# Gate and up products of a SwiGLU from seven block products where eight were formed

## The chip, the cores and the metric

The kernel runs on one core of one Trainium2 chip. Its time is device microseconds (us) from the start to the end of one execution. The engines are TensorE (PE in the profile, its weight loads PEld), VectorE (DVE), ScalarE (ACT), GpSimd (POOL) and SyncE (SP), which here only issues transfers. The operands of products lie in SBUF, the results in the banks of PSUM.

## The reference

One layer of a streaming encoder on 2080 tokens (a prompt of 2048 and a sample of 32) with 1024 features. In front are four mixers between two projections; the change is in what follows them:

```python
        f = rms_norm(x, g_ffn[l])
        hid = jax.nn.silu(jnp.einsum('bld,df->blf', f, w_gate[l])) * jnp.einsum('bld,df->blf', f, w_up[l])
        x = x + jnp.einsum('blf,fd->bld', hid, w_down[l])
...
    y = rms_norm(x, g_final)
```

The hidden width is 2816. All values are float32.

## The kernel before, in words

**Layout.** Features lie on the 128 partitions (8 tiles of 128, `KT`), tokens along the columns, in 5 chunks of 416 (`C`). `x2[c]` holds the running sum of a chunk.

**Exactness.** TensorE takes a format with fewer bits (`F32R`). So every operand is split into a rounded part hi and a rest lo, and `product` (L215 to L223) forms hi·hi, hi·lo and lo·hi: three matmuls of 128 x 128 x 416 for each tile of the contraction, on lines 221, 222 and 223. The hi part of a weight is a ScalarE copy (L128), the lo part a GpSimd subtraction (L129).

**SwiGLU.** The 2816 hidden features are 22 blocks of 128 (`NFB`). `FFN_PASSES` takes chunks 0, 1, 2 in a first pass over all blocks and 3, 4 in a second, so weights are loaded and split twice. For a block and a chunk, `gate` is 24 matmuls and a Silu on ScalarE (L940), `up` 24 matmuls, a VectorE multiplication (L948), a ScalarE copy to hi (L951) and a GpSimd subtraction to lo (L952). `down` is 3 matmuls for each of the 8 output tiles, and VectorE adds each result to `x2` (L862). The downs of a block are queued by `down_later` and issued by `run_downs` between the gates and ups of the next block, a whole gate or more after their operands were begun. Gate, up and down share five PSUM banks (`ps_mm`); three more (`ps_ax`) serve sums.

**What orders the work.** VectorE and TensorE run in the order in which the program is written (`MANUAL`); the other engines' order is chosen by a planner that may move a step ahead. Work that isn't on the way to the next product (norms, statistics, the next chunks' operands) is written as generators in the list `ahead`. After a product the program calls `fill(budget)`, which takes steps from the first `active[0]` generators until their stated VectorE times use up the budget; `WAIT` ends a generator's turn at this product, `LATE` puts a step behind the others. `need` runs what is left of a generator at once.

**Norms.** `ffn_stats` (squares on ScalarE L189, sums on VectorE L190, the sum over partitions by small matmuls L138, a power on GpSimd L154) gives the scale of each token. `spread_far` brings it to all partitions by way of DRAM (L176 out, L178 back). `f_of` makes a chunk's normed hi and lo parts straight from `x2` (L202, L205, L198). `finish` does the last norm of a chunk the same way (L883) and writes it. The last chunk's tokens are taken in two parts of 208 columns (`downs_last`, L905), so that the first part's norm runs beside the second part's products.

## Time and profile before

| | |
|---|---|
| three timed runs | 2201.39, 2204.69 (median), 2205.53 us |
| profiled execution, span from first to last instruction | 2191.8 us, 12.9 under the median |
| mean granted TensorE clock | 0.986 |
| first gate product, end of the last product of SwiGLU | 667.4 us, 2178.3 us |
| PE, DVE, POOL, ACT busy | 2123.2, 1127.5, 696.6, 510.9 us |
| moved by DMA | 147.22 MB, mean 67 GB/s |

The profile gives no separate time of the profiled execution beside its span; what lies around the span is taken as the 12.9 us to the median. In rows by line the columns are: line, engine, operation, result <- operands, shapes, count, then busy time and mean ns of one, then idle time of the engine ahead of them and what ended it. "min/median/max" rows give the spread of one group. Timeline rows give the start, the length, the engine and the line, with the idle time ahead in brackets. A matmul's recorded length (about 350 ns) is longer than its share of the time, since matmuls overlap; the step from one start to the next is what counts.

### The profile page before, as it was taken

To read this page: it belongs to the slowest core of one execution; us is meant where nothing else is said; L and a number is where in the kernel's file an instruction comes from. 1 tells how busy PE (TensorE), PEld (TensorE's weight loads), DVE (VectorE), ACT (ScalarE), POOL (GpSimd) and SP (SyncE) were. 2 spreads that over 40 slices of the span, in tenths; PEclk is the share of its full clock that TensorE was granted. 3 is DMA by queue.
4 is the path that set the end of the run, shared out by engine and by line. 5 is a ranking of instruction groups with operands and counts; after the bars stand their busy time and mean duration, and the time that the engine had idled before them with its cause. 6 is when DMAs were issued, how large, how long until landed. Compare 5 with 4: busy or idle time off the path is not lost.

```text
span 2191.8 us, 27451 instructions
## 1 busy us (share of the span) xinstructions
PE 2123.2 (97%) x11164; PEld 2076.0 (95%) x11164; DVE 1127.5 (51%) x1723; ACT 510.9 (23%) x788; POOL 696.6 (32%) x399
## 2 busy tenths in 40 slices
PE   8799999999889999999999999999999999999998
PEld 7699988899889999999999999999999999999997
DVE  3886598599446433333333333334766533333335
ACT  5324223322423211111111111111322111111123
POOL 2433253243233222222231231232333333333333
PEclk9899999999999999999999999999999999999998
DMA  7534132113321111111111111111122211111111
GB/s 224 165 94 113 63 122 70 48 58 120 113 62 53 39 39 39 39 39 39 39 39 39 39 39 39 39 43 43 48 86 93 93 58 59 59 61 61 60 49 63
DMA packets 54911, 147.22 MB, mean 67 GB/s; under 512 B 14817, under 2 KB 24801, under 8 KB 53633
## 3 DMA queue, kind: packets, MB, share of 16 engines
q1 hardware_dynamic: 52065, 145.29, 20.6%
q8 instruction: 87, 1.43, 0.3%
q10 hardware_dynamic: 2720, 0.18, 0.1%
q14 instruction: 39, 0.32, 0.1%
HBM read 136.77 MB, written 8.68 MB: 66 GB/s over the span
## 4 chain that ended last, share of the span: by engine, by line
PE 80%; DVE 11%; DMA 5%; issue 2%; POOL 1%; ACT 1%; SPq 0%; DVEq 0%; ACTq 0%; POOLq 0%
PE pu L223 7%; PE pu L221 7%; PE pd L222 7%; PE pd L223 7%; PE pg L223 7%; PE pd L221 7%; PE pu L222 7%; PE pg L221 7%; PE pg L222 7%; PE ps L221 4%; PE ps L223 4%; DVE cv L688 4%; PE ps L222 4%; DMA line<-rt 2%; DVE f L202 2%
## 5 line engine op out<-in xcount | busy, mean ns | idle before, releaser
L129 POOL TENSOR_TENSOR wlo<-raw,whi 128x1024 fp32r<-128x1024 f32 x199 | 502.8, 2529 | 854.2 <-ACT whi L128 709.9
L862 DVE TENSOR_TENSOR x<-pd,x 128x416 f32<-128x416 f32 x864 | 491.0, 591 | 432.7 <-PE pd L223 432.7
L221 PE MATMUL pd<-hhi,whi 128*128 128x416 f32 (+1 forms) x896 | 311.2, 347 | 3.0 <-ACT sg L940 2.3
L222 PE MATMUL pd<-hhi,wlo 128*128 128x416 f32 (+1 forms) x896 | 312.8, 349 | 0.0
L223 PE MATMUL pd<-hlo,whi 128*128 128x416 f32 (+1 forms) x896 | 312.1, 348 | 0.2 <-DVE hlo L952 0.2
L223 PE MATMUL pg<-flo,whi 128*128 128x416 f32 x880 | 310.1, 352 | 0.0
L223 PE MATMUL pu<-flo,whi 128*128 128x416 f32 x880 | 309.9, 352 | 0.0
L221 PE MATMUL pu<-fhi,whi 128*128 128x416 f32 x880 | 309.2, 351 | 0.0
L221 PE MATMUL pg<-fhi,whi 128*128 128x416 f32 x880 | 308.9, 351 | 0.0
L222 PE MATMUL pu<-fhi,wlo 128*128 128x416 f32 x880 | 307.8, 350 | 0.0
L222 PE MATMUL pg<-fhi,wlo 128*128 128x416 f32 x880 | 307.5, 349 | 0.0
L128 ACT CAST whi<-raw 128x1024 fp32r<-128x1024 f32 (+1 forms) x205 | 211.9, 1035 | 268.0 <-PE ps L223 111.3
L948 DVE TENSOR_TENSOR sg<-pu,sg 128x416 f32<-128x416 f32 x110 | 65.0, 591 | 396.0 <-PE pu L223 395.9
L952 POOL TENSOR_TENSOR hlo<-sg,hhi 128x416 fp32r<-128x416 f32 x109 | 120.0, 1101 | 436.0 <-ACT hhi L951 435.8
L221 PE MATMUL ps<-hi,whi 128*128 128x416 f32 x640 | 235.6, 368 | 8.3 <-ACT hi L205 4.1
L222 PE MATMUL ps<-hi,wlo 128*128 128x416 f32 x640 | 229.1, 358 | 5.8 <-POOL wlo L129 5.1
L223 PE MATMUL ps<-lo,whi 128*128 128x416 f32 x640 | 230.4, 360 | 2.9 <-POOL lo L198 2.5
L688 DVE SCALAR_TENSOR_TENSOR cv<-z,par,cv 128x416 f32<-128x416 f32 (+2 forms) x180 | 209.9, 1226 | 1.0 <-ACT cv L682 0.8
L951 ACT CAST hhi<-sg 128x416 fp32r<-128x416 f32 x110 | 59.5, 541 | 596.4 <-DVE sg L948 587.9
L221 PEld LDWEIGHTS pd<-hhi,whi 128*128 128x128 f32 x896 | 168.4, 188 | 6.9 <-ACT sg L940 3.0
L223 PEld LDWEIGHTS pd<-hlo,whi 128*128 128x128 f32 x896 | 168.3, 188 | 1.8 <-DVE hlo L952 0.3
L222 PEld LDWEIGHTS pd<-hhi,wlo 128*128 128x128 f32 x896 | 168.3, 188 | 1.5
(140 smaller groups left out, 2719.7 us busy)
## 6 DMA issues: line engine op xcount, KB each, us to landing
raw<-in_w_gate SPq DMA_DIRECT2D x44, 512.0 KB
raw<-in_w_up SPq DMA_DIRECT2D x44, 512.0 KB
raw<-in_w_down SPq DMA_DIRECT2D x44, 512.0 KB
raw<-in_w_in SPq DMA_DIRECT2D x43, 512.0 KB
raw<-in_w_out SPq DMA_DIRECT2D x24, 512.0 KB
xt<-in_xt SPq DMA_DIRECT2D x20, 416.0 KB
x<-in_x SPq DMA_DIRECT2D x5, 1664.0 KB
xk<-in_x SPq DMA_DIRECT2D x32, 208.0 KB
```

Of the source, the lines that this page charges most:

```text
L128: nc.scalar.copy(out=hf[:, o], in_=raw[:, o])
L129: lo_eng.tensor_sub(out=lf[:, o], in0=raw[:, o], in1=hf[:, o].bitcast(F32))
L202: nc.vector.scalar_tensor_tensor(out=f, in0=x(k), scalar=col(gname, k), in1=r[:, :C], op0=ALU.mult, op1=ALU.mult)
L221: nc.tensor.matmul(out, whi, xhi, start=start and k == 0, stop=False)
L222: nc.tensor.matmul(out, wlo, xhi, start=False, stop=False)
L223: nc.tensor.matmul(out, whi, xlo, start=False, stop=stop and k == n - 1)
L688: nc.vector.scalar_tensor_tensor(out=cv[:, t, :n], in0=z[:, t, j : j + n], scalar=col("w_conf", 31 * t + j), in1=cv[:, t, :n], op0=ALU.mul ...
L862: nc.vector.tensor_add(out=x2[c][:, m], in0=ps[:, :C], in1=x2[c][:, m])
L948: nc.vector.tensor_mul(out=sg, in0=ps[:, :C], in1=sg)
L951: nc.scalar.copy(out=hi, in_=sg)
L952: lo_eng.tensor_sub(out=lo, in0=sg, in1=hi.bitcast(F32))
```

## The change

The gate and the up projection of two feature blocks and two token chunks together are a product of 2 x 2 blocks: the 1024 inputs in two halves (`H` = 4 tiles each), the outputs in two blocks of 128, the tokens in two chunks. Formed plainly that is eight block products. The change forms seven (p1 to p7), of sums and differences of the weight blocks and of the operand's blocks, and puts the four results together from them.

- The tokens are cut into six chunks of 346 to 348 (`FCH`), in three passes of two; so weights are loaded and split three times.
- `operands` makes the seven weight operands of a pair of feature blocks: four sums of 512 columns on VectorE, seven splits (ScalarE, GpSimd). They are made three products ahead (`LEAD`).
- `halves` makes the seven operands of the tokens: four scalings and four differences per tile on VectorE, seven splits whose lo parts alternate between GpSimd and VectorE. The normed rows are read back from DRAM (`x2d`), where `ffn_stats` now stores `x2`. In the first pass the parts of p3 are made last, because their place is free only when the mixers' buffers are closed. The operands of the second and third pass are made when all pairs of the pass before are written, beside its last 16 downs.
- `block` forms the seven products in four PSUM banks. p2, p3 and p4 are added in PSUM onto p1, p5 and p7, after VectorE or ScalarE has read those. `evac` is called for each of the four quadrants; three of them add a partial sum (`u2`, `u3`) on VectorE.
- `up` multiplies three quadrants on GpSimd, and the lo part of all four is now a VectorE subtraction.
- `down` contracts both feature blocks into one bank: six matmuls and one VectorE addition. Downs now use the three banks of `ps_ax`. `DOWNS` says how many follow each of the 14 products of a pair; the first follows the first product.
- The running sum of a pass (`residual`) is loaded from `x2d` after the first pair of that pass, into the buffers of the two chunks before, after these have been finished.
- The end is rewritten: the last two chunks' downs follow one another, the first one's `finish` is filled in beside the second one's downs, and the second's norm follows.

The core of the diff:

```diff
+FCH = (348, 348, 346, 346, 346, 346)
...
+FPASSES = ((0, 1), (2, 3), (4, 5))
+NG = NFB // 2
+H = KT // 2
+ORDER = ("p1", "p5", "p7", "p6", "p2", "p3", "p4")
+DOWNS = (1, 1, 2, 1, 1, 2, 1, 1, 2, 1, 1, 2, 0, 0)
+LEAD = 3
...
-FFN_PASSES = ((0, 1, 2), (3, 4))
...
+    x2d = dramp.tile([P, KT, T], F32, tag="x2d", name="x2d", bufs=1)
...
+        nc.sync.dma_start(out=x2d[:, :, c * C : (c + 1) * C], in_=x2[c])
...
+    def halves(p):
+        for c in STATS_OF[p]:
+            need(("fstats", c))
+        n = FCH[FPASSES[p][0]]
+        r = []
+        for c in FPASSES[p]:
...
+        yield WAIT
+        f[p] = {}
+        engs = [nc.gpsimd, nc.vector]
+        def split(name, kk, src):
...
+            nc.scalar.copy(out=hi[:, kk, :n], in_=src)
+            engs[0].tensor_sub(out=lo[:, kk, :n], in0=src, in1=hi[:, kk, :n].bitcast(F32))
+            engs.append(engs.pop(0))
+        def normed(i, k):
+            c = FPASSES[p][i]
+            x = rowf("xf")[:, :n]
+            nc.sync.dma_start(out=x, in_=x2d[:, k, FO[c] : FO[c] + n])
+            nc.vector.scalar_tensor_tensor(
+                out=x, in0=x, scalar=col("g_ffn", k), in1=r[i][:, :n], op0=ALU.mult, op1=ALU.mult
+            )
+            return x
+        for kk in range(H):
+            f11 = normed(0, kk)
+            yield 0.8
+            split("p1", kk, f11)
+            f12 = normed(1, kk)
+            yield 0.8
+            t1 = rowf("t1")[:, :n]
+            nc.vector.tensor_sub(out=t1, in0=f12, in1=f11)
+            split("p5", kk, t1)
+            yield 1.0
+            f22 = normed(1, kk + H)
+            yield 0.8
+            t2 = f11
+            nc.vector.tensor_sub(out=t2, in0=f22, in1=t1)
+            t3 = t1
+            nc.vector.tensor_sub(out=t3, in0=f22, in1=f12)
+            split("p7", kk, t3)
+            yield 1.6
+            split("p6", kk, t2)
+            f21 = normed(0, kk + H)
+            yield 1.2
+            split("p2", kk, f21)
...
+            t4 = f12
+            nc.vector.tensor_sub(out=t4, in0=f21, in1=t2)
+            split("p4", kk, t4)
+            yield 1.0
+        if p == 0:
+            yield HOLD
+            for kk in range(H):
+                f22 = normed(1, kk + H)
+                yield 0.8
+                split("p3", kk, f22)
...
+    early = itertools.takewhile(lambda s: s is not HOLD, made["f", 0])
+    ahead.append(early)
+    for _ in w_out_pass(2):
+        pass
+    for _ in early:
+        pass
...
+    mixers.close()
+    f3 = ctx.enter_context(tc.tile_pool(name="f3", bufs=1, reuse_waits="tile"))
...
+    fw = ctx.enter_context(tc.tile_pool(name="fw", bufs=5, reuse_waits="tile"))
+    hidp = ctx.enter_context(tc.tile_pool(name="hidp", bufs=10, reuse_waits="tile"))
...
+    def weight_parts(src, tag="w", **bufs):
+        hi = fw.tile([P, H, P], F32R, tag=tag + "hi", name="whi", **bufs)
+        lo = fw.tile([P, H, P], F32R, tag=tag + "lo", name="wlo", **bufs)
...
+        nc.scalar.copy(out=hf, in_=src)
+        nc.gpsimd.tensor_sub(out=lf, in0=src, in1=hf.bitcast(F32))
+        return hi, lo
+    def operands(src, g):
+        r1, r2 = raw_of(src, g, 0), raw_of(src, g, 1)
+        a11, a21, a12, a22 = r1[:, 0], r1[:, 1], r2[:, 0], r2[:, 1]
...
+        yield weight_parts(a11)
+        s1 = total(a21, a22, add=True)
+        yield weight_parts(s1)
+        yield weight_parts(total(a11, a21))
+        s2 = total(s1, a11)
+        yield weight_parts(s2)
+        yield weight_parts(a12)
+        yield weight_parts(total(a12, s2))
+        yield weight_parts(a22)
...
+        def take(self, step):
+            self.upto(step + LEAD)
+            return self.done.pop(step)
...
+    def wide(w, x, n, ps, start, stop):
...
+        for k in range(H):
+            nc.tensor.matmul(ps, whi[:, k], xhi[:, k, :n], start=start and k == 0, stop=False, **more)
+            nc.tensor.matmul(ps, wlo[:, k], xhi[:, k, :n], start=False, stop=False, **more)
+            nc.tensor.matmul(ps, whi[:, k], xlo[:, k, :n], start=False, stop=stop and k == H - 1, **more)
...
+    def down(c, m, w, hid):
+        n = FCH[c]
+        ps = ps_ax.tile([P, 512], F32, tag="ax", name="pd")[:, :n]
+        for i, ((whi, wlo), (hhi, hlo)) in enumerate(zip(w, hid)):
+            nc.tensor.matmul(ps, whi[:, m % H], hhi[:, :n], start=i == 0, stop=False)
+            nc.tensor.matmul(ps, wlo[:, m % H], hhi[:, :n], start=False, stop=False)
+            nc.tensor.matmul(ps, whi[:, m % H], hlo[:, :n], start=False, stop=i == 1)
+        nc.vector.tensor_add(out=xs[c][:, m, :n], in0=ps, in1=xs[c][:, m, :n])
...
+    def block(p, evac):
+        n = FCH[FPASSES[p][0]]
+        bank = {}
+        def out(name):
+            bank[name] = ps_mm.tile([P, 512], F32, tag="mm", name="pw")[:, :n]
+            return bank[name]
+        def form(name, ps, start, stop):
+            w = wq.take(step[0])
+            wide(w, f[p][name], n, ps, start, True)
+        def then(k):
+            run_downs(DOWNS[step[0] % 14])
+            step[0] += 1
+        form("p1", out("a"), True, False)
+        fill(0.9)
+        r1 = rowf("r1")[:, :n]
+        nc.scalar.copy(out=r1, in_=bank["a"])
+        then(0)
+        form("p5", out("d"), True, False)
+        fill(1.0)
+        then(1)
+        form("p7", out("e"), True, False)
+        fill(0.6)
+        then(2)
+        form("p6", out("b"), True, True)
+        fill(0.6)
+        u2 = rowf("u2")[:, :n]
+        nc.vector.tensor_add(out=u2, in0=bank["b"], in1=r1)
+        u3 = rowf("u3")[:, :n]
+        nc.vector.tensor_add(out=u3, in0=bank["e"], in1=u2)
+        evac((1, 1), bank["d"], u3)
+        then(3)
+        form("p2", bank["a"], False, True)
+        fill(0.3)
+        evac((0, 0), bank["a"], None)
+        then(4)
+        form("p3", bank["d"], False, True)
+        fill(0.6)
+        evac((0, 1), bank["d"], u2)
+        then(5)
+        form("p4", bank["e"], False, True)
+        fill(0.6)
+        evac((1, 0), bank["e"], u2)
+        then(6)
+    def ffn_pair(p, g):
...
+        def gate(q, ps, plus):
+            s = rowf("sg")[:, :n]
+            if plus is not None:
+                nc.vector.tensor_add(out=s, in0=ps, in1=plus)
+                ps = s
+            nc.scalar.activation(out=s, in_=ps, func=AF.Silu)
+            sg[q] = s
+        def up(q, ps, plus):
+            s = sg[q]
+            if plus is not None:
+                u = rowf("up")[:, :n]
+                nc.vector.tensor_add(out=u, in0=ps, in1=plus)
+                nc.gpsimd.tensor_mul(out=s, in0=u, in1=s)
+            else:
+                nc.vector.tensor_mul(out=s, in0=ps, in1=s)
+            hi = hidp.tile([P, FN], F32R, tag="hid", name="hhi")
+            lo = hidp.tile([P, FN], F32R, tag="hid", name="hlo")
+            nc.scalar.copy(out=hi[:, :n], in_=s)
+            nc.vector.tensor_sub(out=lo[:, :n], in0=s, in1=hi[:, :n].bitcast(F32))
+            hid[q] = hi, lo
+        block(p, gate)
+        block(p, up)
+        return hid
...
+        order = [(m, i) for m in range(KT) for i in range(2)]
+        if by_chunk:
+            order = [(m, i) for i in range(2) for m in range(KT)]
+        for m, i in order:
+            downs.append(
+                lambda m=m, i=i: down(FPASSES[p][i], m, wd(m // H), [hid[0, i], hid[1, i]])
+            )
...
+    def finish(c):
+        n = FCH[c]
+        x = xs[c]
+        acc = rowf("ssum")
+        whole(acc, n)
+        for k in range(KT):
+            sq = acc if k == 0 else rowf("sq")
+            nc.scalar.activation(out=sq[:, :n], in_=x[:, k, :n], func=AF.Square)
+            if k:
+                nc.vector.tensor_add(out=acc[:, :n], in0=acc[:, :n], in1=sq[:, :n])
+            yield 0.8
+        yield WAIT
+        tok = ps_ax.tile([P, 512], F32, tag="ax", name="tok")
+        for j in range(FNB):
+            sums(tok[:FTB, j : j + 1], acc, j)
+        yield LATE
+        rt = token_scales([tok[:FTB, :FNB]])
+        yield WAIT
+        line = dramp.tile([FNB, FTB], F32, tag="line2", name="line")
+        nc.sync.dma_start(out=line.rearrange("j q -> q j"), in_=rt[:FTB, :FNB])
+        r = rowf("rs")
+        nc.sync.dma_start(out=r, in_=line.rearrange("(o j) q -> o (j q)", o=1).broadcast_to([P, FN]))
         yield WAIT
         yield WAIT
...
         for k in range(KT):
...
+            nc.vector.scalar_tensor_tensor(
+                out=x[:, k, :n], in0=x[:, k, :n], scalar=col("g_final", k), in1=r[:, :n],
+                op0=ALU.mult, op1=ALU.mult,
+            )
+            yield 0.8
+        nc.sync.dma_start(out=a["y"][:, :, FO[c] : FO[c] + n], in_=x[:, :, :n])
...
+    def residual(p):
+        for c in FPASSES[p]:
+            xs[c] = bigp.tile([P, KT, FN], F32, tag="big", name="xs")
+            nc.sync.dma_start(out=xs[c][:, :, : FCH[c]], in_=x2d[:, :, FO[c] : FO[c] + FCH[c]])
+    last = len(FPASSES) - 1
+    wq.upto(2)
+    for c in PASSES[2]:
+        start(("fstats", c), ffn_stats(c))
+    for p in range(len(FPASSES)):
+        need(("f", p))
+        for g in range(NG):
+            hid = ffn_pair(p, g)
+            if g == 0:
+                if p:
+                    need(*(("finish", c) for c in FPASSES[p - 1]))
                 else:
+                    need(*(("fstats", c) for c in PASSES[2]))
+                residual(p)
+            wd = down_later(p, g, hid, by_chunk=p == last and g == NG - 1)
+            wd(0)
+        if p < last:
+            made["f", p + 1] = halves(p + 1)
+            ahead.insert(0, made["f", p + 1])
+            active[0] = 1
+            while downs:
+                run_downs(1)
+                fill(2.0)
+            for c in FPASSES[p]:
+                start(("finish", c), finish(c))
...
+    ahead.append(finish(ca))
...
+    for m in range(KT):
+        run_downs(1)
...
+        fill(1.2)
...
+    for _ in iter(lambda: fill(100.0) or bool(ahead), False):
```

369 lines of the change are left out of this document (150 added, 219 removed).

## The prediction

> **What bounds the kernel now.** I read the header and the busy shares first, then the slices and the chain of waits.
>
> ```profile
> span 2191.8 us, 27451 instructions
> PE 2123.2 (97%) x11164; PEld 2076.0 (95%) x11164; DVE 1127.5 (51%) x1723; ACT 510.9 (23%) x788; POOL 696.6 (32%) x399
> PE 80%; DVE 11%; DMA 5%; issue 2%; POOL 1%; ACT 1%; SPq 0%; DVEq 0%; ACTq 0%; POOLq 0%
> 640.00:1560.00 920.00, 920.00 (x4879) 910.59 (x4878) 378.76 (x646) 163.28 (x248) 250.30 (x145) 1.00 0.12 41
> ```
>
> TensorE is busy 97% of the span and makes 80% of the chain. The last row is a stretch of the feed-forward part (columns: length, then PE, PEld, DVE, ACT and POOL busy, granted clock, DMA share, GB/s): not one idle moment in 920 us at full clock, while VectorE works 41% and GpSimd 27%. A product there costs 920 / 4879 = 0.1886 us. So products set the time of this stage, and the other engines have room in the mean. Fewer columns mean less time, if nothing else comes to sit on PE's path. The whole question is the second half of that sentence.
>
> **Products.** Gate and up are 880 x 6 products of 416 columns, down 7920 - 5280 = 2640 more.
>
> ```profile
> L223 PE MATMUL pg<-flo,whi 128*128 128x416 f32 x880 | 310.1, 352 | 0.0
> 2170.16 0.27 PE L221 MATMUL pd<-hhi,whi 128*128 128x208 f32 x1
> ...
> 2172.73 0.28 PE L223 MATMUL pd<-hlo,whi 128*128 128x208 f32 x1
> ```
>
> The count of 7920 is 22 feature blocks x 5 chunks x 72, or 7920 x 0.1886 = 1494 us. After: per pass and pair of feature blocks 2 x 7 x 12 = 168 gate and up products and 16 x 6 = 96 down products, x 33 = 8712, of 346 to 348 columns. Their price is not shown. The two ends of the timeline of 208-column products are 24 products, 23 steps apart: 2.57 / 23 = 0.1117 us. The line through 208 and 416 gives 0.163 at 347; scaling 0.1886 by width gives 0.157. I take 0.161: 8712 x 0.161 = 1403, a saving of **91 us** (74 by the line, 126 by the width).
>
> The Trainium skill, "TensorE: Matmul & The Clock Gate", section "Wait — 56ns, not 53.3ns?", puts a warm step at columns / 2.4 GHz + 2.5 ns. As an estimate by that page the two counts would be 1392 and 1281 us, 111 saved; the rows above are longer at both widths, so the rows decide.
>
> **What the added work costs elsewhere.** By form:
>
> ```profile
> L129 POOL TENSOR_TENSOR wlo<-raw,whi 128x1024 fp32r<-128x1024 f32 x199 | 502.8, 2529 | 854.2 <-ACT whi L128 709.9 <-PE pd L222 109.9 <-PE pd L223 17.3
> L376 POOL TENSOR_TENSOR wlo<-raw,whi 128x256 fp32r<-128x256 f32 x4 | 3.4, 847 | 8.7 <-ACT whi L375 8.7
> L952 POOL TENSOR_TENSOR hlo<-sg,hhi 128x416 fp32r<-128x416 f32 x109 | 120.0, 1101 | 436.0 <-ACT hhi L951 435.8
> L1032 POOL TENSOR_TENSOR sq<-sq 128x208 f32<-128x208 f32 x5 | 3.0, 634 | 0.1
> L862 DVE TENSOR_TENSOR x<-pd,x 128x416 f32<-128x416 f32 x864 | 491.0, 591 | 432.7 <-PE pd L223 432.7
> L905 DVE TENSOR_TENSOR x<-pd,x 128x208 f32<-128x208 f32 x16 | 5.8, 373 | 4.3 <-PE pd L223 4.3
> L129 DVE TENSOR_TENSOR wlo<-raw,whi 128x512 fp32r<-128x512 f32 x6 | 3.9, 684 | 1.1 <-ACT whi L128 1.1
> L128 ACT CAST whi<-raw 128x512 fp32r<-128x512 f32 x6 | 3.4, 617 | 2.0 <-PE ps L223 1.5 <-DMA raw<-in_w_in 0.5
> L951 ACT CAST hhi<-sg 128x416 fp32r<-128x416 f32 x110 | 59.5, 541 | 596.4 <-DVE sg L948 587.9 <-PE pd L222 8.4
> ```
>
> Between those widths: a GpSimd operation of 512 costs 1.41 us and of 347 0.95; VectorE 0.68 at 512 and 0.52 at 347; ScalarE 0.62 at 512 and, by width, 0.48 at 347. Per pair of blocks PE needs 264 x 0.161 = 42.5 us. GpSimd: 18 weight parts x 1.41 + 3 x 0.95 = 28. VectorE: 8 weight sums x 0.68, 4 partial sums, 3 gate adds, 4 up steps, 4 low parts and 16 down additions at 0.52: 22. ScalarE: 18 x 0.62 + 10 x 0.48 = 16. Nothing is over 42.5, so no engine is the bound in the mean. But VectorE and GpSimd now meet:
>
> ```profile
> L190 DVE TENSOR_TENSOR ssum<-ssum,sq x63: 577/592/2601, 470.1 to 2157.9; 128x416 f32<-128x416 f32 x63
> L862 DVE TENSOR_TENSOR x<-pd,x x864: 573/592/593, 700.2 to 2153.2; 128x416 f32<-128x416 f32 x173
> 1557.21 1.13 POOL L952 TENSOR_TENSOR hlo<-sg,hhi 128x416 fp32r<-128x416 f32 x1 [0.27 <-ACT hhi L951]
> 1557.31 1.47 DVE L198 TENSOR_TENSOR flo<-f,fhi 128x416 fp32r<-128x416 f32 x1
> ```
>
> The additions that read PSUM never exceed 593 ns; those that read two SBUF tiles have the same median and a maximum of 2601. The one at 1557.31 ends 0.44 after GpSimd's operation: it waited for it. Weight sums and low parts are of that kind.
>
> **The wait for hid, once per pair.** VectorE and PE run in written order. In the new up, each of three quadrants goes VectorE add, GpSimd multiply, ScalarE copy, VectorE subtract, and the subtract stands in VectorE's queue ahead of the next quadrant, weight sum and down additions. The first down of a pair follows one product (1.93 us) after the last quadrant's, and its fourth matmul needs that quadrant's parts, 2.4 us after p4 ends.
>
> ```profile
> 1009.18 2.25 DVE L862 TENSOR_TENSOR x<-pd,x 128x416 f32<-128x416 f32 x4
> 1009.35 0.54 ACT L951 CAST hhi<-sg 128x416 fp32r<-128x416 f32 x1 [6.70 <-DVE sg L948]
> 1009.97 1.09 POOL L952 TENSOR_TENSOR hlo<-sg,hhi 128x416 fp32r<-128x416 f32 x1 [4.83 <-ACT hhi L951]
> ```
>
> The hop from ScalarE's end (1009.89) to GpSimd is 0.08; I use 0.09. From the end of p6: two partial sums and the add to 1.8; multiply, copy, subtract to 4.0; one down addition, the next quadrant's multiply, copy and subtract to 6.1; two down additions and a weight sum to 7.6; add, multiply, copy, subtract to 10.3; a weight sum, then the last quadrant's four to 13.5. PE's p4 ends at 0.97 + 1.93 + 1.93 + 1.93 + 1.93 = 8.7, and it needs the result at 11.1 to 11.5: a stall of 2.05 us with every engine free when asked. With GpSimd 28 / 46 busy, six two-SBUF operations wait 0.3 each and three multiplies 0.3: 4.85. If VectorE had no backlog at all, the last four steps alone take 2.75: 0.35. I take the middle of 2.05 and 4.85, **3.5 us x 30 = 105 us** (33 pairs less three ends of a pass; ends 10 and 146).
>
> A stall can cost more than its length:
>
> ```profile
> 476.83 0.89 PE L138 MATMUL tok<-ones,ssum 128*104 128x1 f32 x8 [4.05 <-DVE ssum L190]
> 478.00:482.00 4.00, 4.00 (x15) 3.84 (x14) 4.00 (x5) 0.00 (x0) 0.00 (x0) 0.61 0.23 89
> ```
>
> After 4.05 us of idleness the clock of the next 4 us was 0.61. Losing 0.39 x 4 = 1.6 us on 30 stalls would be 47 more; as mine are 3.5, I take none and keep 47 in the range. By the Trainium skill, "TensorE: Matmul & The Clock Gate", section "What's actually happening", the clock halves after an idle window of about 3.4 us; half of such stalls would then pay, an estimate of 24 us.
>
> **Starts and ends of passes.** The chain's rows and others:
>
> ```profile
> 573.40 4.01 DMA rs<-line
> 1609.35 5.89 DMA line<-rt
> 1615.73 5.19 DMA raw<-in_w_gate
> L154 POOL TENSOR_TENSOR rt<-ms,mhalf 104x4 f32<-104x4 f32 x19 | 20.5, 1079 | 88.6 <-DVE ms L148 88.6
> L883 DVE SCALAR_TENSOR_TENSOR x<-x,par,rs 128x416 f32<-128x416 f32 x24 | 20.8, 925 | 0.0
> L883 DVE SCALAR_TENSOR_TENSOR x<-x,par,rs x24: 635/644/2800, 1624.5 to 1724.0; 128x416 f32<-128x416 f32 x24
> 2172.00:2174.00 2.00, 2.00 (x20) 2.00 (x19) 0.98 (x3) 0.76 (x2) 1.31 (x4) 1.00 1.02 426
> ```
>
> *Start of passes 2 and 3.* fill gives the finish steps 9.2 us in the first pair, the two chunks cost 25.6. The rest is forced: seven scalings at 0.56 and seven dependent square sums at 0.62, 8.3 us, behind the last hid (4.8 after p4); PE's token sums stand ahead of the next products, so PE idles 13. Then GpSimd's power (1.1), the line out and back (5.9 + 4.0) and eight scalings (4.5) hold VectorE's queue, then the output and the reload of 1.4 MB each into the same buffer at 426 GB/s (6.7): 22 us, against which PE has three products and three downs, 8.7. Sum 13 + 13, less the ordinary 3.5: 23; I take **25 each, 50**, (15 to 35), and **5** (0 to 8) for the first pass, whose reload waits for no output.
>
> *Ends of passes 1 and 2.* The next chunks' parts are made beside 16 downs (15.5 us of PE). Per k VectorE has four scalings (0.56), four differences and 3.5 low parts (0.52): 6.1, x 4 = 25; L883's mean is 925 against a median of 644, so x 1.35 with GpSimd beside it: 33. With 16 additions at 0.44: 40. PE idles 24 and 4.8 for hid; I take **27 each, 54** (21 to 35). PE's first product needs the last k, so no product covers it.
>
> *Start of SwiGLU.* The weights' new buffers lie where w_out's operands were: a load (5.2), a cast (0.6), a low part (1.4), hops, then half clock (1.6): **9** (5 to 13). The mixers' own stretch gets stores of x and the new operands beside it: 0 (-5 to +10), as VectorE's last 60 us there are budgeted.
>
> *The end.* Of chunk 5's norm the line out and back (9.9), eight scalings (4.5), then the diagonal, its product, six scalings and the output, some 9, follow the last product: 23.
>
> ```profile
> 2177.89 0.41 PE L223 MATMUL pd<-hlo,whi 128*128 128x208 f32 x1
> ```
>
> Before, 13.5 followed (2191.8 - 2178.3). With hid's 4.8, less about 4 of PE's gaps there: **+10** (5 to 20).
>
> **Sum.** -91 + 105 + 50 + 5 + 54 + 9 + 10 = +142: span 2334. The median lies 12.9 over the profiled span (2204.7 - 2191.8), so **2347 us**.
>
> **Rivals.** *Faster:* the hid chain meets PE's own backlog, and finish and operands overlap. Hid 0, starts 15, ends 20, 11 for SwiGLU's start and the end: -91 + 46 = -45, **2160** (2120 to 2195). For it: room on every engine; against it: written order leaves PE nothing else to issue. *GpSimd becomes the bound:* it decides from 46 us a pair, that is about 2.4 us a part. At 2.53, the price of the double width, 18 x 2.53 + 3 x 1.1 = 48.8, x 33 = 1610 against 1494, with 50 + 5 + 54 + 9 + 10: +244, **2449**. Against it: 847 ns at 256. *Products don't get cheaper with width:* 8712 x 0.1886 = 1643, 240 more than in my sum, **2587**; 0.1117 at 208 speaks against it. That the change forms eight products after all is read from the count.
>
> **Chances.** Mine 0.65 (own range 2222 to 2440: all low ends but the bare chain, and some two thirds of the high ends, as they won't come together), GpSimd 0.07, width 0.02: slower 0.74. Faster rival 0.22. Between the two, within 0.2% (4.4 us, about what a measurement of this kernel can tell from no change): 0.04. Both signs count, so the range goes down to 2150, through most of the faster rival, and up to 2440.
>
> **What would show it.** PE busy near 1403 us over SwiGLU; 5544 products into the gate and up banks with a step near 0.161; PE idle some 3 to 4 us per pair in front of the first down, released by VectorE's low part; gaps over 20 us behind the first pair of passes 2 and 3 and at their joins. If PE is at 97% and those gaps are absent, I am wrong on the waits; if the step is 0.188, on the products; if PE waits for GpSimd's weight parts throughout, the second rival has it.

## The result and the profile after

The changed kernel takes 2477.39 us (median of 4 runs, 2475.69 to 2481.05), the kernel before on the same chip 2205.11 (2201.39 to 2208.22): a ratio of 1.1236, interval 1.1219 to 1.1252. It is 272 us slower, where 142 were forecast. Its profiled execution took 2478.6 us, 1.7 more than its span, and the runs beside the experiments have the same 1.7. So the 12.9 us that were taken as lying around the span of the kernel before were not that: its profiled execution must have been a faster one, of some 2193.5 us. Against that trace the difference is 285 us, and the traces have to account for those. The page of the profiled execution begins:

```profile
span 2476.9 us, 30874 instructions
PE 2143.8 (87%) x11900; PEld 2076.0 (84%) x11900; DVE 1396.2 (56%) x2103; ACT 764.2 (31%) x1396; POOL 1160.5 (47%) x883
...
PEclk9899989999989999999986999999987889999996
...
PE 57%; DVE 20%; DMA 9%; POOL 5%; issue 5%; ACT 4%; SPq 0%; DVEq 0%; ACTq 0%; POOLq 0%
```

TensorE was busy 97% of the span and is at 87%; its share of the chain fell from 80% to 57%, and what it lost went to VectorE, the DMA and GpSimd. No engine has become the bound: VectorE and GpSimd are about half busy. The clock row dips where passes join (86 in the middle, 8788 later) and at the end.

Stretches of the trace (length, then PE, PEld, DVE, ACT and POOL busy with counts, granted clock, DMA share, GB/s): all of SwiGLU, and one pair from after its waits to its end.

```profile
692.20:2452.60 1760.40, 1516.40 (x8781) 1482.25 (x8782) 902.97 (x1472) 540.99 (x1040) 917.66 (x744) 0.92 0.23 72
...
985.60:1024.00 38.40, 38.40 (x241) 38.40 (x241) 19.51 (x33) 11.68 (x22) 20.25 (x17) 0.99 0.21 65
```

The second row gives the price of a product in the new kernel: 38.40 / 241 = 0.1593 us (0.1594 over many pairs, which is used below). 8712 of them are 1389 us. SwiGLU takes 1760. So the products did become cheaper, by 105 us, and 372 us came on top. They lie at the joints, where one pair of feature blocks ends and the next begins, at the ends and the starts of passes, and at the end; the mixers in front took longer too.

**At the joint of every pair.** The timeline around one joint, with the rows that bear on the wait; the copies `r<-pw` on ScalarE stand behind the first product of a block, so the two rows of this kind are one pair apart.

```profile
977.04 1.08 DVE L1120 TENSOR_TENSOR hlo<-sg,hhi 128x348 fp32r<-128x348 f32 x1 [1.57 <-ACT hhi L1119]
...
977.23 0.45 ACT L1068 COPY r<-pw 128x348 f32<-128x348 f32 x1 [0.22 <-PE pw L1026]
977.30 0.32 PE L1038 MATMUL pd<-hlo,whi 128*128 128x348 f32 x1
...
978.05 0.68 DVE L976 TENSOR_TENSOR sum<-raw 128x512 f32<-128x512 f32 x1
978.65 0.51 DVE L1113 TENSOR_TENSOR up<-pw,u 128x348 f32<-128x348 f32 x1
...
979.24 0.92 POOL L1114 TENSOR_TENSOR sg<-up,sg 128x348 f32<-128x348 f32 x1 [1.49 <-DVE up L1113]
...
980.19 0.48 ACT L1119 CAST hhi<-sg 128x348 fp32r<-128x348 f32 x1 [0.81 <-POOL sg L1114]
980.72 0.43 PE L1036 MATMUL pd<-hhi,whi 128*128 128x348 f32 x1 [3.11 <-ACT hhi L1119]
...
981.82 0.43 PE L1038 MATMUL pd<-hlo,whi 128*128 128x348 f32 x1 [0.51 <-DVE hlo L1120]
...
982.09 0.32 PE L1024 MATMUL pw<-f_p,whi 128*128 128x348 f32 x1
...
1025.03 0.45 ACT L1068 COPY r<-pw 128x348 f32<-128x348 f32 x1 [0.22 <-PE pw L1026]
```

A pair is 1025.03 - 977.23 = 47.80 us; its 264 products are 42.1. Of the 5.7 beyond, TensorE waits 3.11 for the hi part of the last quadrant of hid and 0.51 for its lo part. The rows above the wait show the chain: VectorE sits 1.57 us in front of the quadrant before's lo subtraction, subtracts, sums weights, and only then adds p4's quadrant (978.65), which GpSimd, ScalarE and TensorE await in turn. From start to start the two waits cost 4.1 us (977.30 to 982.09, less four steps of 0.16). The rest is the clock behind them:

```profile
982.20:985.20 3.00, 3.00 (x14) 3.00 (x13) 0.61 (x2) 1.14 (x2) 1.99 (x2) 0.58 0.51 156
985.20:989.20 4.00, 4.00 (x25) 4.00 (x24) 1.12 (x2) 1.29 (x3) 1.11 (x2) 0.89 0.06 18
```

0.42 x 3.0 + 0.11 x 4.0 = 1.7 us. The group of the first matmuls of downs has the same wait over the whole trace: of 160.9 us of idle time ahead of it, 98.3 ended with hid's hi part. They are 31 waits: 27 joints with 3.08 to 3.11 us each, the first joint with 1.7, and the ends of the three passes with 3.0 to 5.0.

```profile
L1036 PE MATMUL pd<-hhi,whi 128*128 128x346 f32 (+1 forms) x1056 | 366.8, 347 | 160.9 <-ACT hhi L1119 98.3
```

**At the ends and starts of passes.** Three stretches, from the last pair of the first pass to the second pair of the next:

```profile
1166.20:1256.10 89.90, 69.75 (x362) 65.12 (x361) 56.97 (x93) 29.09 (x57) 45.70 (x38) 0.85 0.26 80
1256.10:1313.30 57.20, 32.00 (x182) 30.00 (x181) 38.52 (x60) 22.31 (x48) 29.35 (x23) 0.80 0.25 73
1313.30:1380.50 67.20, 48.26 (x266) 47.52 (x267) 24.06 (x44) 12.63 (x24) 22.80 (x18) 0.82 0.36 111
```

By the program they hold 360, 168 and 264 gate, up and down products, 57.4, 26.8 and 42.1 us. The first is 32.5 over that, the two others together 55.5. Where TensorE stands still for long in the latter two, two rows of VectorE, and the chain of waits there (start, length, what):

```profile
1301.20 0.58 DVE L1194 SCALAR_TENSOR_TENSOR xs<-xs,par,rs 128x348 f32<-128x348 f32 x1 [3.21 <-DMA rs<-line]
1301.70 0.51 DVE L1113 TENSOR_TENSOR up<-pw,u 128x346 f32<-128x346 f32 x1
...
1312.13 1.32 PE L1162 MATMUL tok<-ones,ssum 128*116 128x1 f32 x6 [19.41 <-DVE ssum L1178]
...
1335.49 0.66 PE L1036 MATMUL pd<-hhi,whi 128*128 128x346 f32 x1 [11.58 <-DVE xs L1039]
...
1348.41 0.66 PE L1036 MATMUL pd<-hhi,whi 128*128 128x346 f32 x1 [7.36 <-DVE xs L1039]
```

```profile
1308.27 5.84 DMA out_y<-xs
...
1314.72 11.68 DMA line<-rt
...
1326.44 3.92 DMA rs<-line
...
1334.43 6.66 DMA out_y<-xs
...
1341.12 6.53 DMA xs<-x2d
```

First the second chunk's token sums, then its line through DRAM, then its output, then the load into the buffer that the output frees. One reason why the token sums are so late: VectorE's order has the first chunk's first scaling, which waits 3.21 us for its row from DRAM, ahead of p4's addition (1301.70). That addition comes some 9 us after p4's last product, where it comes 3.6 after it at an ordinary joint. The line of 1.4 KB takes 11.68 us where the first chunk's took 6.7: SyncE issued it at 1314.72, 0.6 us behind the load of 1.4 MB for the first chunk. The Trainium skill, "DMA: Bandwidth & Descriptors", section "Queues, rings and completion order", says that each DMA engine consumes the descriptors of its ring in order; the trace agrees, as the line lands 12.3 us after that load's issue, about when the load (6.5) and a line's own time (5.9 in the kernel before) are over.

**At the end.** The chain around the last downs but one (rows of 0.1 us or less between are left out):

```profile
2441.47 0.53 DVE xs L1039
2442.03 0.49 ACT sq L1246
...
2444.07 0.44 DVE xs L1039
2444.53 0.50 ACT sq L1246
2445.17 0.92 POOL sq L1248
2446.14 0.77 PE tok L1162 x6
...
2450.77 6.55 DMA line<-rt
```

Token sums of the last chunk stand in TensorE's order right behind its downs, each behind VectorE's addition, ScalarE's square and GpSimd's sum.

**In the mixers.** The last 180 of the 2880 products of the mixers' projections took 33.6 us before and 43.5 after:

```profile
643.70:687.20 43.50, 37.72 (x180) 35.97 (x179) 31.65 (x45) 13.70 (x26) 19.00 (x13) 0.92 0.44 109
```

### The profile page after: what moved, and what is told of

Same layout as the page of the kernel before. It is cut to its first block, busy times and chain, and to the rows that moved or that the text cites. A ratio compares the mean times of both kernels' runs of the same rounds, so it can differ in the third digit from the quotient of the medians.

```text
span 2476.9 us, 30874 instructions
## 1 busy us (share of the span) xinstructions
PE 2143.8 (87%) x11900; PEld 2076.0 (84%) x11900; DVE 1396.2 (56%) x2103; ACT 764.2 (31%) x1396; POOL 1160.5 (47%) x883
## 4 chain that ended last, share of the span: by engine, by line
PE 57%; DVE 20%; DMA 9%; POOL 5%; issue 5%; ACT 4%; SPq 0%; DVEq 0%; ACTq 0%; POOLq 0%
PE pw L1025 9%; PE pw L1026 9%; PE pw L1024 9%; PE pd L1038 7%; PE pd L1036 6%; PE pd L1037 6%; PE ps L233 3%; PE ps L231 3%; PE ps L232 3%; DVE hlo L1120 3%; DVE cv L703 3%; DMA line<-rt 3%; POOL sg L1114 3%; DVE sum L976 2%; ACT hhi L1119 2%
## 5 line engine op out<-in xcount | busy, mean ns | idle before, releaser
L1024 PE MATMUL pw<-f_p,whi 128*128 128x346 f32 (+1 forms) x1848 | 614.0, 332 | 17.2 <-ACT whi L965 13.0
L1025 PE MATMUL pw<-f_p,wlo 128*128 128x346 f32 (+1 forms) x1848 | 614.5, 333 | 5.0 <-POOL wlo L966 5.0
L1026 PE MATMUL pw<-f_p,whi 128*128 128x346 f32 (+1 forms) x1848 | 614.6, 333 | 1.8 <-POOL f_p L884 1.6
L966 POOL TENSOR_TENSOR wlo<-sum,whi 128x512 fp32r<-128x512 f32 x264 | 344.2, 1304 | 529.5 <-ACT whi L965 276.1
L1036 PE MATMUL pd<-hhi,whi 128*128 128x346 f32 (+1 forms) x1056 | 366.8, 347 | 160.9 <-ACT hhi L1119 98.3
L966 POOL TENSOR_TENSOR wlo<-raw,whi 128x512 fp32r<-128x512 f32 x330 | 448.1, 1375 | 110.4 <-ACT whi L965 110.4
L1024 PEld LDWEIGHTS pw<-f_p,whi 128*128 128x128 f32 x1848 | 364.5, 197 | 20.0 <-ACT whi L965 14.1
L1038 PE MATMUL pd<-hlo,whi 128*128 128x346 f32 (+1 forms) x1056 | 361.2, 342 | 13.1 <-DVE hlo L1120 12.3
L1025 PEld LDWEIGHTS pw<-f_p,wlo 128*128 128x128 f32 x1848 | 364.1, 197 | 6.5 <-POOL wlo L966 6.5
L1026 PEld LDWEIGHTS pw<-f_p,whi 128*128 128x128 f32 x1848 | 365.4, 198 | 2.9 <-POOL f_p L884 2.2
L1037 PE MATMUL pd<-hhi,wlo 128*128 128x346 f32 (+1 forms) x1056 | 356.5, 338 | 0.0
L139 POOL TENSOR_TENSOR wlo<-raw,whi 128x1024 fp32r<-128x1024 f32 x67 | 183.3, 2740 | 285.7 <-ACT whi L138 285.7
```

The costliest lines, as they stand in the source:

```text
L966: nc.gpsimd.tensor_sub(out=lf, in0=src, in1=hf.bitcast(F32))
L1024: nc.tensor.matmul(ps, whi[:, k], xhi[:, k, :n], start=start and k == 0, stop=False, **more)
L1025: nc.tensor.matmul(ps, wlo[:, k], xhi[:, k, :n], start=False, stop=False, **more)
L1026: nc.tensor.matmul(ps, whi[:, k], xlo[:, k, :n], start=False, stop=stop and k == H - 1, **more)
L1036: nc.tensor.matmul(ps, whi[:, m % H], hhi[:, :n], start=i == 0, stop=False)
L1037: nc.tensor.matmul(ps, wlo[:, m % H], hhi[:, :n], start=False, stop=False)
```

## The experiments

Each is the changed kernel with the edit shown, timed once, the last one four times. Beside them the kernel before took 2198.87, 2196.53, 2197.36 and 2197.39 us, 6 to 9 less than beside the changed kernel; so lengths within the traces decide more than totals. "Pair" is the time from one `r<-pw` to the next but one, in the middle of a pass; "excess" is a stretch's length, from first product to first product, less 0.1594 us for each of its products.

### What holds up the joint of a pair

**e1_downs**

```diff
-DOWNS = (1, 1, 2, 1, 1, 2, 1, 1, 2, 1, 1, 2, 0, 0)
+DOWNS = (0, 0, 2, 2, 2, 2, 2, 2, 1, 1, 1, 1, 0, 0)
```

> The downs of a pair begin behind the third product of the next pair and not behind the first. Theory (VectorE's written order): the last hid part is ready 3.3 us too late for a down behind the first product, so two more products (3.8 us) cover it, and without the idle time the clock is not halved. A pair takes 42.5 to 43.5 us in place of 47.8, thirty pairs some 140 us less, 2330 to 2345 in all. Rival (the engines behind the products are at their limit, GpSimd's weight parts above all): PE waits elsewhere instead, a pair stays above 46 us and the time above 2430.

2371.89 us, a pair of 44.6. The wait for hid is gone and the clock whole, but 2.5 us stay, which neither theory had. TensorE's waits at one joint:

```profile
1039.56 0.42 PE L1025 MATMUL pw<-f_p,wlo 128*128 128x348 f32 x1 [0.46 <-POOL wlo L966]
...
1043.20 0.43 PE L1025 MATMUL pw<-f_p,wlo 128*128 128x348 f32 x1 [1.48 <-POOL wlo L966]
```

With no downs between, the next two products come so early that the lo parts of their weight sums are not there. The clock of the 3 us behind these waits was 1.00.

**e7_downs_lead**: the same, and `LEAD = 4`.

> The first experiment (no down behind the first two products of a gate block), and in addition the weight operands are made four products ahead where it was three. Theory: what was left of the pair's excess there (44.6 us where 264 steps of 0.1594 are 42.1) is the wait for lo parts of weight sums that stand behind up's subtractions in VectorE's written order; written one product earlier they stand ahead of them, and a pair takes 42.2 to 43 us, the kernel 2305 to 2330. Rival: VectorE and GpSimd are simply late by then, whatever the order; the pair stays at 44 us or more and the kernel at 2355 or above.

2370.02 us, a pair of 44.7: the rival's numbers held, though not its reason, since e13_best below brings the pair down by order alone. The second of those waits is gone and the wait for hid is back (0.82 for a weight part, 0.46 for hid's hi part, 0.52 for its lo part at the joint near 1002). VectorE's order is one line: what is moved ahead in it pushes the quadrants back.

**e3_extra**: 16 useless products into a bank of their own, behind the first product of each pair that has downs.

```diff
+EXTRA = 16
...
+    warm_w = fw.tile([P, P], F32R, tag="warmw", name="warm_w", bufs=1)
+    nc.scalar.copy(out=warm_w, in_=ones)
...
+        if downs and step[0] % 14 == 0:
+            extra = ps_mm.tile([P, 512], F32, tag="mm", name="extra")
+            hi = f[p]["p1"][0]
+            for i in range(EXTRA):
+                nc.tensor.matmul(extra[:, :n], warm_w, hi[:, i % H, :n], start=True, stop=True, skip_group_check=True)
```

> Sixteen products of constants (2.6 us) are added behind the first product of each pair but a pass's first, into a PSUM bank of their own: work that nobody needs, in the place where PE stands idle for 3.3 us. Theory (the idle time halves the clock afterwards): PE is never idle for over 1 us there, the half clock of 3.4 us per pair goes, and a pair takes 1.5 to 1.7 us less although it has sixteen products more: 46.2 us, about 2430 in all. Rival (the half clock has another cause, or the idle time is not what it seems): a pair takes the same or up to 2.6 us more, 2477 to 2550.

2419.72 us, a pair of 46.3: 1.5 us less, by adding work, as the theory said. Behind the joint the clock is whole:

```profile
1011.00:1014.00 3.00, 3.00 (x20) 3.00 (x20) 0.65 (x2) 1.01 (x2) 2.38 (x2) 1.00 0.53 175
```

Same 3.0 us as above, 20 products where there were 14. So the clock behind the joint drops because of the idle time (0.58 with it, 1.00 with useless products in its place), and this part of the 5.7 us is 1.5 to 1.7.

**e2_lo_pool**

```diff
-            nc.vector.tensor_sub(out=lo[:, :n], in0=s, in1=hi[:, :n].bitcast(F32))
+            nc.gpsimd.tensor_sub(out=lo[:, :n], in0=s, in1=hi[:, :n].bitcast(F32))
```

> The low part of hid is made by GpSimd, as in the kernel before, and not by VectorE; the downs stay where they are. Theory (VectorE's written order): VectorE no longer stands waiting for GpSimd and ScalarE ahead of the next quadrant, so the last quadrant's add runs as soon as its product ends; the low part is ready some 3.5 us after that product in place of 6, the stall falls from 3.3 to about 1, the clock stays whole, a pair takes 43 to 44.5 us, 2370 to 2400 in all. Rival (it is the chain of four steps itself, or GpSimd's load, that is too long): the stall stays at 3 us or grows, and the time is 2470 or more.

2548.62 us, a pair of 51.2: the rival held. VectorE was freed, and p4's addition started 0.2 us after p4's last product, at 979.20. But GpSimd multiplied that quadrant only at 982.94, behind weight parts in its own queue, so the hi part came nearly as late as in the changed kernel, and the lo part, behind two more weight parts, almost as long again after it.

```profile
984.42 0.66 PE L1036 MATMUL pd<-hhi,whi 128*128 128x348 f32 x1 [2.87 <-ACT hhi L1119]
...
988.11 0.66 PE L1038 MATMUL pd<-hlo,whi 128*128 128x348 f32 x1 [2.74 <-POOL hlo L1120]
```

**e11_defer**: VectorE keeps the subtraction, but it stands behind the next quadrant's addition.

```diff
+        late = []
...
-            nc.vector.tensor_sub(out=lo[:, :n], in0=s, in1=hi[:, :n].bitcast(F32))
+            if late:
+                late.pop()()
+            late.append(lambda: nc.vector.tensor_sub(out=lo[:, :n], in0=s, in1=hi[:, :n].bitcast(F32)))
             hid[q] = hi, lo
+            if len(hid) == 4:
+                late.pop()()
```

> Only VectorE's written order changes: the lo subtraction of a quadrant of the hidden values stands behind the next quadrant's addition, not ahead of it. Theory: in the changed kernel the addition for p4 starts at 978.65, about 3 us after p4's last product, because VectorE first waits 1.57 us for the hi part of the quadrant before and then subtracts and sums; GpSimd's multiplication, ScalarE's cast and the first down all stand behind this. With the addition at about 975.5 the hi part is there near 978, TensorE's wait of 3.1 us falls to about 0.5, the clock stays whole, and a pair takes 43 to 44 us where it took 47.8: the kernel 2350 to 2380. Rival: GpSimd's queue of weight parts then sets the multiplication, as in the run where it took the lo parts; the pair stays at 46 us or more and the kernel above 2415.

2401.99 us, pairs of 45.1 and 46.7: between theory and rival. The waits are 1.73 and 0.83. p4's addition comes 1.6 us after p4's last product, where it was some 3.6. GpSimd then multiplies p3's and p4's quadrants one behind the other (2.27 us from 955.16), as it was at weight parts until then. So VectorE's order is a little under half of the wait for the hi part (3.11 to 1.73), and GpSimd's queue stands in the rest. The two lengths differ by the clock alone: behind the same two waits, it was 0.64 behind one pair and 1.00 behind the next.

```profile
913.40:916.40 3.00, 3.00 (x14) 3.00 (x14) 0.71 (x2) 1.14 (x2) 1.89 (x2) 0.64 0.43 145
960.20:963.20 3.00, 3.00 (x20) 3.00 (x20) 0.67 (x3) 1.14 (x2) 2.04 (x2) 1.00 0.47 160
```

**e12_order**: for each output tile, the second chunk's down first.

```diff
-        order = [(m, i) for m in range(KT) for i in range(2)]
+        order = [(m, i) for m in range(KT) for i in (1, 0)]
```

> Only the order of the downs changes: for each output tile the second chunk's down stands first. The second chunk's hidden values come from p6 and p3, the first chunk's from p2 and p4, the last of all. Theory: the first down then waits for p3's quadrant, about 3.6 us earlier by the trace (hi part at 977.0 against 980.7), so that wait is under 1 us, and the second down, behind one more product, comes at about 980 and waits up to 1.5 us: a pair takes 43.5 to 45.5 us and the kernel 2365 to 2420. Rival: what delays the last quadrant isn't the order but the engines' load, and the wait only moves to the next down in full: pair 47 us or more.

2340.91 us, a pair of 43.4, the best of the single edits and a little better than the theory's 43.5 to 45.5. Nothing became faster: p4's addition still comes 3.6 us after p4's last product. The first down only takes the quadrants that are ready first, and the others are there, but for 0.2 us, when the second down asks. The one longer wait at the joint, and the copies at both ends of a pair:

```profile
1033.70 0.42 PE L1038 MATMUL pd<-hlo,whi 128*128 128x348 f32 x1 [0.52 <-DVE hlo L1120]
```

```profile
989.39 0.45 ACT L1068 COPY r<-pw 128x348 f32<-128x348 f32 x1 [0.24 <-PE pw L1026]
...
1032.76 0.45 ACT L1068 COPY r<-pw 128x348 f32<-128x348 f32 x1 [0.22 <-PE pw L1026]
```

30 pairs x 4.4 = 132 us. The load of every engine is the same here, so the wait came from the order in which the downs ask for the quadrants.

### What holds up the start of a pass

Excess of the first two pairs of passes 2 and 3, in the changed kernel: 55.5 and 57.7 us.

**e4_finish**: in the first pair of those passes, 1.2 more filled in behind each product, from two generators.

```diff
+    more = [0.0]
...
+            fill(more[0])
...
+            more[0] = 1.2 if p and g == 0 else 0.0
+            active[0] = 2 if p and g == 0 else active[0]
...
+            if p:
+                active[0] = 1
```

> In the first pair of passes 2 and 3 each product gets 1.2 us more of the finish steps, of both chunks in turn, so that little of them is left to be forced behind that pair. Theory (the starts of passes are long because norms, the way out to DRAM and back, the output and the reload follow one another behind the first pair): the 50 us each that these starts lose fall to about 20, 2410 to 2425 in all. Rival (output and reload of 1.4 MB each way are what takes the time, whatever comes ahead): no more than 10 us gained each, 2455 or more.

2454.81 us; excess 50.4 and 54.3, so 5 and 3 us less: the rival held. Less forced work ahead of the token sums did not shorten the rest of the chain: the second line still went out 1.4 us behind the load of the first chunk and took 11.8 us.

**e8_pieces**: output and load by two of the eight tiles.

```diff
-        nc.sync.dma_start(out=a["y"][:, :, FO[c] : FO[c] + n], in_=x[:, :, :n])
+            if k % 2:
+                nc.sync.dma_start(out=a["y"][:, k - 1 : k + 1, FO[c] : FO[c] + n], in_=x[:, k - 1 : k + 1, :n])
...
-            nc.sync.dma_start(out=xs[c][:, :, : FCH[c]], in_=x2d[:, :, FO[c] : FO[c] + FCH[c]])
+            for k in range(0, KT, 2):
+                nc.sync.dma_start(out=xs[c][:, k : k + 2, : FCH[c]], in_=x2d[:, k : k + 2, FO[c] : FO[c] + FCH[c]])
```

> The output of a finished chunk and the load of the next running sum go in four pieces of two tiles each, not in one transfer of 1.4 MB, so that the first pieces leave while VectorE still scales. Theory: output and load in series (6.7 + 6.5 us) stand at the end of the chain on which the second pair of passes 2 and 3 waits; they shrink to about 6 us, and the length of the first two pairs beyond 42.1 us each, together 55.5 and 57.7 us, falls to 45 to 50, the kernel by 14 to 20 us. Rival: the chain is set by what stands ahead of it (forced token sums, the line's way through DRAM); the pieces then only queue the second chunk's line deeper and nothing is gained.

2441.51 us; excess 44.1 and 44.1. The theory held, just past its better end (45): 11 and 14 us less. The first two pairs of the second pass:

```profile
1247.60:1303.90 56.30, 32.01 (x182) 30.07 (x181) 38.50 (x60) 22.32 (x48) 29.37 (x23) 0.80 0.27 81
1303.90:1360.60 56.70, 47.31 (x265) 46.58 (x266) 24.31 (x44) 12.52 (x24) 22.80 (x18) 0.87 0.38 125
```

The first is as long as it was; the second is 10.5 shorter. From the last scaling (1322.3) to the first addition into the new sum (1329.3) it is 7 us, where it was 13.4. The second line, issued 3.7 us behind the first piece of the load, took 8.7 us: again it landed 12.4 us after that load began.

**e9_lock**: both edits above, and the two finishes run by turns where they are forced.

```diff
-                    need(*(("finish", c) for c in FPASSES[p - 1]))
+                    for _ in itertools.zip_longest(*(made["finish", c] for c in FPASSES[p - 1])):
+                        pass
```

> Three edits of the passes' starts together: more of the two finishes is filled in behind the products of the first pair, their steps are run by turns (both lines go out ahead of the first output), and output and load go in pieces as in the run beside this one. Theory: at the start of a pass TensorE waits for one chain after another: token sums, line out and back, scaling, output, load, and of the second chunk's line again behind the first's load; with the two chunks side by side one such chain is left, of about 5.9 + 4.0 us for the line, 8 for 16 scalings and 5 for the last pieces; the first two pairs' excess falls from 55 and 58 us to 25 to 30 each, the kernel by 50 to 60. Rival: the transfers' bandwidth sets it (5.6 MB of outputs and loads, about 26 us in each pass); then no less than 45 us is left.

2427.82 us; excess 41.1 and 40.5, where 25 to 30 was expected and the rival said 45. Both fell. The chains still stood one behind the other: the second line went out at 1288.46, behind the first chunk's load (1283.82), since by the time of the forced turns the first finish was far ahead. VectorE's waits for transfers in that start:

```profile
1272.52 1.07 DVE L1197 SCALAR_TENSOR_TENSOR xs<-xs,par,rs 128x348 f32<-128x348 f32 x2 [6.92 <-DMA rs<-line]
...
1301.35 1.56 DVE L1197 SCALAR_TENSOR_TENSOR xs<-xs,par,rs 128x348 f32<-128x348 f32 x3 [8.85 <-DMA rs<-line]
...
1319.09 0.52 DVE L1039 TENSOR_TENSOR xs<-pd,xs 128x346 f32<-128x346 f32 x1 [6.54 <-DMA xs<-x2d]
```

What a start with one line and not two in series would cost was not tried, nor a line on another queue.

### The end

**e5_tail**

```diff
+    held = []
+
+    def held_sums():
+        k, q = held.pop(0)
+        for j in range(FNB):
+            sums(toks[j], q, j, k == 1, k == 7)
...
         if m in (1, 3, 5, 6, 7):
-            for j in range(FNB):
-                sums(toks[j], sq, j, m == 1, m == 7)
+            held.append((m, sq))
+        if m in (4, 6):
+            held_sums()
+    while held:
+        held_sums()
```

> The token sums of the last chunk, which TensorE takes right behind each down, are written later: the sum of the first two squares behind the fifth down, that of the next two behind the seventh, the others behind the last. Theory: the four gaps of 3.8, 3.5, 3.5 and 1.7 us in TensorE's last pair are waits for the chain add, square, add in front of each sum; about 10 us of them go and the end from the last pair on falls by 8 to 12 us. Rival: VectorE and ScalarE set the pace of the last downs (additions into the running sum, squares of the chunk before, scalings), then the gaps move to the end and at most 4 us are gained.

2453.17 us. The last pair's excess, up to the start of its last product, fell from 31.3 to 20.3: 11 us, as the theory said. What follows took 23.2 us; it was 24.3 in the changed kernel, but 22.1 to 23.2 in the other runs above that leave this part alone, so nothing was gained there.

### The mixers

**e14_vec**: in the first pass all lo parts of the token operands on VectorE.

```diff
-        engs = [nc.gpsimd, nc.vector]
+        engs = [nc.vector, nc.vector] if p == 0 else [nc.gpsimd, nc.vector]
```

> In the first pass the lo parts of the tokens' operands are all made by VectorE, where GpSimd made every other one. Theory: the first gate product came later than before because products of the mixers' last output pass wait for weight lo parts on GpSimd behind these subtractions; without them the first gate product is 5 to 10 us earlier than in the runs beside this one. Rival: VectorE's own work (operands, additions into the sums) sets the end of that stage; then the start is no earlier, or later by up to 10 us.

2463.73 us; the first gate product came at 683.9, in the run of e11_defer, where this stage is unchanged, at 682.3. The rival held. TensorE's longest waits between 630 and 690 us, in the changed kernel and then in this run (what waits, for what; us, times, longest):

```profile
PE ps L232 <- POOL wlo L139: 4.4, 2, 2.2
...
PE ps L231 <- DVE x L353: 7.2, 4, 3.8
```

Relieved of this work, GpSimd is no longer waited for in the mixers, and VectorE is, in its additions into the sum.

**e15_late**: the first pass's operands are not filled in beside the mixers' last output pass.

```diff
-    ahead.append(early)
     for _ in w_out_pass(2):
```

> The token operands of the first pass are not filled in beside the mixers' last output pass, but made in one go behind it. Theory: that pass is stretched because VectorE adds each of its results behind a chain scaling, cast, lo part of the new operands, whatever engine makes the lo parts; without them its last 180 products take 34 us, as in the kernel before, where they take 41 to 43, and the last product of the mixers comes 8 us earlier, at about 669; the first gate product then waits for the operands and comes some 25 us later than before, at 700 to 715. Rival: the pass is stretched by the stores of x and the loads of rows on the queue, which stay; then its last product comes at 674 or later.

2485.05 us. The last mixer product came at 665.4, where e11_defer has 677.3, and its last 180 products took 33.8 us, as in the kernel before (33.6), where e11_defer has 41.4:

```profile
631.60:665.40 33.80, 33.80 (x181) 33.51 (x179) 4.15 (x7) 3.21 (x4) 4.80 (x2) 1.00 0.18 69
```

So the operands beside that pass stretch it by about 8 us. By e14 it matters little which engine makes the lo parts; the loads of rows moved away here too, so their share is not separated. The first gate product came at 670.2, not at 700 to 715; the wait came behind it, as the first pair's excess was 52.6 us, where it is 16.6 in the changed kernel. So the early operands are worth their 8 us.

### Together

**e13_best**: e7's `DOWNS` and `LEAD`, e11's order, e9's three edits, e5's.

> All that helped, together: no down behind the first two products of a gate block, the weight operands four products ahead, the lo subtraction of a quadrant behind the next addition, finishes filled in more and side by side, output and load in pieces, token sums of the last chunk held back. Theory: an ordinary pair is at its products' time, 42.1 to 42.6 us (30 x 5.3 = 160 us less), the starts of passes 2 and 3 give 30 us and the end 11: about 2270 to 2290, still slower than the kernel before by 70 to 90 us, of which the ends of passes 1 and 2 are 54. Rival: with the pairs shorter VectorE and GpSimd have no slack, a pair stays at 44 us and the kernel above 2320.

2266.32 us (median of 4, 2263.42 to 2268.04) against 2197.36 before (7 runs): a ratio of 1.0318, interval 1.0299 to 1.0337. The theory held, with 4 us to spare. The swapped order of e12 is not in it; the two together were not run. A pair is 42.7 us at full clock, the products' time and 0.6:

```profile
1009.40:1052.10 42.70, 42.37 (x266) 42.03 (x265) 25.99 (x39) 14.67 (x29) 27.50 (x21) 1.00 0.22 75
```

What is left against the kernel before is at the passes: ends of passes 1 and 2 with an excess of 26.8 and 27.2, starts of 2 and 3 with 37.1 and 35.8, the start of the first with 19, the last pair with 12.6.

## Why the prediction was right on the direction and short by half

In the two profiled executions the changed kernel costs 285 us more (2476.9 - 2191.8). By the prediction's terms, first what it said and then what the trace has:

| term | predicted | measured |
|---|---|---|
| products | -91 | -105 (8712 x 0.1594 against 7920 x 0.1886) |
| joint of a pair, 30 times | +105 | +171 (5.7 each) |
| starts of passes 2 and 3 | +50 | +102 (55.5 + 57.7, less two ordinary joints) |
| start of pass 1 | +5 | +17 |
| ends of passes 1 and 2 | +54 | +54 (32.5 + 32.4, less two joints) |
| mixers and start of SwiGLU | +9 | +25 (first gate product 692.2, was 667.4) |
| the end | +10 | +36 (31.3 less a joint, and 24.3 where 13.9 followed) |
| left out | 0 | -17 (the kernel before's own time beyond its products), +3 in single pairs |

They add up to 286. The joints stayed below the high end that the prediction gave them (146, and 47 for the clock); the starts of passes 2 and 3 (at most 70) and the end (at most 20) did not.

- **Right: the direction, its cause, and the products.** PE had nothing else to issue at the joints, as argued, and idles where it was said: in front of the first down, and at the joins of passes. The price by the two widths was 0.161 against 0.1594.
- **Right in size: the wait for hid.** 3.11 + 0.51 us where the middle of two bounds gave 3.5. That it fell on the middle is partly luck: the bounds were 2.05 and 4.85 (by the terms named, 4.75). The chain was that of the prediction, except that most of the wait ends with ScalarE's hi part and not with VectorE's lo part: e12 and e11 shorten it by order alone, and e2 shows GpSimd's queue in it.
- **Wrong: "as mine are 3.5, I take none".** The halved clock behind the wait was priced (47 us for 30 stalls), kept in the range and left out of the sum, because the row at hand had 4.05 us of idleness and mine was shorter. It came at every ordinary joint (pairs of 47.7 to 49.0 us, none shorter once the first two are past) and cost 1.5 to 1.7 us, by e3: 45 to 51 us, most of the 66 by which this term was short. The rest is that two waits of 3.6 us cost 4.1 from start to start. By the rule of the Trainium skill that the prediction cites ("TensorE: Matmul & The Clock Gate", section "What's actually happening") half of the stalls would pay, an estimate of 24 us; the runs show that all did.
- **Wrong in size: "25 each".** PE's idleness in front of the token sums was put at 13 and was 19.4: the first chunk's scaling stood ahead of p4's addition and waited for its row, which the sum did not have. Then the sum took 5.9 us for the second chunk's line and 6.7 for output and load together, both at 426 GB/s; the trace has 11.7 for the line, and 6.7 and 6.5 us for output and load of 1.4 MB each, about half that rate. e8 shows the latter by taking 11 to 14 us away. That the second line is slow because of the load ahead of it is read from the traces (it landed 12.3 us after that load's issue here and 12.4 in e8, though issued 0.6 and 3.7 us behind it); no run moved that load alone. About 17 of the 55 us are shorter waits and the clock (0.80 and 0.82 in the two stretches), which the sum had left out here too. The start of the first pass (17 where 5 was taken) has waits for weight parts on GpSimd (3.2 us), for quadrants on VectorE (3.8) and for token sums (3.1), none of which was in the sum.
- **Wrong in size: "+10" for the end.** The line and the scalings behind the last product were as said; the token sums between the last downs were put at 4 us of gaps, and e5 takes out 11. The rest has the clock of the last pair in it, 0.85 on average.
- **Wrong: "0" for the mixers.** VectorE had room in the mean there, as the prediction says, but the operands made beside that pass hold it up by 8 us (e15). Of the 25 in this profile, 5 arose before any changed instruction ran: the 1401st product of the mixers starts at 311.2 us where it started at 306.0 before. Another 5 came between that and the last 180 products and are not explained; in the experiments' runs with the operands in their place the first gate product came at 679 to 685, not at 692. The start of SwiGLU itself was 5 us, where 9 was taken.
- **Right in size, partly by luck: the ends.** 27 each was the sum over VectorE's operations with its slower two-SBUF ones, and 26.8 is what was there. But TensorE waits 11.4 us for VectorE there, not 24, at a clock of 0.69 between 1219.6 and 1256.1. And the prediction let the next pass's first product wait for the last tile's operands, but it starts at 1256.1 while VectorE is at them until 1266. No run tested this.
- **The rivals.** The faster one needed the joints to vanish; e13 shows that they can (42.7 us a pair) and that the kernel would still be slower, because of the passes. GpSimd did not become the bound: its weight parts took 1.30 to 1.38 us on average, where 2.4 would have been needed.

With all its high ends the prediction's sum would have reached some 2515 us; the range, up to 2440, gave part of that up because the high ends would not come together. They mostly did: the lowered clock is part of the joints, the starts and the end alike.

## What to carry to other kernels

Fewer products buy nothing while their results pass through three engines, one of them in written order, just ahead of the product that needs them: look for the consumer first, and give it the results in the order in which they become ready (one swapped loop turned 272 us over the kernel before into 144). Count a stall of TensorE with the clock that it costs behind it, once for each stall: here waits of 3.6 us in all paid every time, of 2.6 (e11) about every other time, and of 1.9 (e1) not. Where a buffer is written out and loaded anew, price the two transfers one behind the other, price whatever small transfer is issued behind them on the same queue, and cut them into pieces.

## What the runs showed of the hardware

- Useless products in front of a wait made the kernel faster: 16 of them shortened a pair from 47.8 to 46.3 us.
- The same two waits (1.73 and 0.83 us) halved the clock behind them in some pairs and not in others (0.64 and 1.00). The Trainium skill, "TensorE: Matmul & The Clock Gate", section "What's actually happening", says that the window in which activity is counted runs freely; that would fit, but no run here shows where the window stood.
- A line of 1.4 KB took 11.7 us when issued 0.6 us behind a transfer of 1.4 MB, 8.7 when issued 3.7 us behind the start of the same in four pieces, and 5.9 to 6.7 alone.
